# A hybrid attention and SSD layer: the product with V divided by the sums, another interleaving, and row transfers from ScalarE

## The chip, the cores and the metric

The kernel runs on one core of a Trainium2 chip. Its engines work side by side, each on its own queue of instructions in order: TensorE (PE; PEld is its weight load), VectorE (DVE), ScalarE (ACT), GpSimd (POOL) and SyncE (SP), which here only issues transfers. Operands lie in SBUF, the results of TensorE in the eight banks of PSUM. The metric is the device time of one execution in microseconds (us); the kernel before takes 1001.02 us, the median of three runs from 999.69 to 1004.33.

## The reference

One layer of a diffusion backbone: 512 latent tokens and 256 context tokens of width 1024, in float32. The parts that matter here:

```python
def attend(q_nope, q_rope, k_nope, k_rope, v):
    s = (jnp.einsum("bqhd,bkhd->bhqk", q_nope, k_nope)
         + jnp.einsum("bqhr,bkr->bhqk", q_rope, k_rope)) * ATTN_SCALE
    p = jax.nn.softmax(s.astype(jnp.float32), axis=-1).astype(v.dtype)
    return jnp.einsum("bhqk,bkhd->bqhd", p, v)
...
        attn_x = latent_attention(q_nope_x, q_rope_x,
                                  jnp.concatenate([k_nope_c, k_nope_x], axis=1),
                                  jnp.concatenate([kr_c, k_rope_x], axis=1),
                                  jnp.concatenate([v_c, v_x], axis=1))
...
        y_x = ssd_output(st_xf[0], st_xf[1]) + flip(ssd_output(st_xb[0], st_xb[1]))
        ssd_x = ssd_finish(y_x, xs_x, z_x, ssd_d[l], ssd_norm[l])

        mix_x = jnp.concatenate([attn_x, ssd_x], axis=-1) @ w_out[l]
        x = x + mod_x[2] * rms_norm(mix_x, mix_post_norm[l])
        ffn_x = conv_glu(modulate(rms_norm(x, ffn_pre_norm[l]), mod_x[3], mod_x[4]),
                         w_up[l], ffn_conv_w[l], ffn_conv_b[l], w_down[l])
        x = x + mod_x[5] * rms_norm(ffn_x, ffn_post_norm[l])
```

There are 16 heads of attention, 512 queries against 768 keys each, and an SSD (a scan in chunks of 128, in both directions) in two groups of heads; both feed one output projection, and a gated MLP follows.

## The kernel before

Large products are made from pairs of tiles: `split` (L495) rounds an operand to its high part on ScalarE (L497) and takes the rest on VectorE (L498), and three products of the parts stand for one. Tokens are cut in blocks of 128 rows.

The program goes through the input projections (`xbc`, `latent`; `gemm_T` at L751), the SSD (`ssd`, `ssd_finish`), attention in eight pairs of heads (`project`, `pair_of_heads`), the output projection (`natural_gemm`, L1289), the MLP's way up (L751 again) and its way down (L1476).

**SSD.** For each group a recurrence runs over six chunks in two directions: POOL multiplies the inputs by weights (L1005), TensorE multiplies (L1010), POOL multiplies the state of the chunk before by its decay (L1014), VectorE adds (L1015). Then come the masks (L1025 to L1039) and the outputs (L1044 to L1063). `ssd_finish` scales the rows and transposes them (L1082).

**Attention.** `project` makes q, k and v of a pair of heads; SP moves them from partitions to partitions (L1150 to L1156). For each block of 128 queries of a head, `scores` makes 128 x 768 scores in PSUM (L1175), VectorE takes the negative maximum of each row (L1177), ScalarE the exponential and each row's sum (L1179), VectorE the reciprocal of the sum (L1181), POOL multiplies the 768 columns by it (L1182). `transposed` turns the six blocks in PSUM (L1193, two banks) and splits them; `weighted` multiplies with V (L1205), in a form in which the result has the 64 dims of the head on partitions and the queries along the row. That is copied and added into the tile of the pair (L1229, L1230).

**Modulation.** The rows that scale the output projection and the MLP's input come from products with a weight of 1024 x 1024 each (`modblock`, VectorE at L586, eight transfers of 512 KB). `modfinish` has each as a column of 8 values on 128 partitions, writes it to DRAM (L1276, 1024 words) and reads it back as a row, copied to all partitions (L1278). Both transfers are issued by POOL. The first two rows belong to the output projection (`after_mix`, L1354 and L1373), the third to the end.

**Order.** The code is run once to record its instructions, and a planner (`plan`, `Graph`) then orders each engine's instructions by their distance to the end, priced by a table of its own, and gives every tile its place in SBUF: `UNITS` pieces of 256 words per partition, four to a block. A tile's place must be free in the order of the code, and the planner prefers places that came free earlier by `MARGIN`. `beside` (L453) sets the order of the code: it runs the SSD (`group_sums`) as the main line and the projections and attention (`projections`) beside it, and `pace` says how much of the second goes with a given amount of the first. What is left of the second runs alone afterwards.

## Time and profile before

| what | value |
| --- | --- |
| median of three runs | 1001.02 us (999.69 to 1004.33) |
| span of the profiled execution | 994.4 us, 14412 instructions (the page lists no time of its own for it) |
| TensorE clock granted, mean | 0.990 |
| read from HBM, written | 96.02 MB, 4.21 MB |
| GpSimd at L1182 | 64 instructions, 97.3 us |
| ScalarE busy | 501.4 us |

The span goes from the first to the last instruction. A busy engine has an instruction in work; ends of matmuls are modelled, so they overlap, and a busy TensorE is not one at its peak. The granted clock is the share of full speed that TensorE is given. In groups of instructions a row has line, engine, operation, output and inputs by the program's names, shapes, count, busy us, mean ns of one, and the idle time before them with what ended it. In waits a row has who waited for whom, us in total, times, the longest.

### The profile page before, as it was taken

The numbers are of one execution on the slowest core, as the hardware profiler recorded it, in microseconds if no ns is written. First come the engines' busy times: TensorE is split into PE (matmuls) and PEld (weight loads), VectorE is DVE, ScalarE is ACT, GpSimd is POOL, SyncE is SP. The second block draws the span as 40 slices with busy tenths as digits, with TensorE's granted clock in tenths as the row PEclk, the third lists the DMA queues.
The fourth block names the chain that finished last, engine by engine and source line by source line (L and its number), as shares of the span: only waits on it lengthen the run. The fifth ranks groups of instructions, "written<-read, shape, count | busy, mean of one in ns | idle before, by whom it ended". The sixth has DMA issues, their size and how long they took to land.

```text
span 994.4 us, 14412 instructions
## 1 busy us (share of the span) xinstructions
PE 971.8 (98%) x5224; PEld 825.9 (83%) x5224; DVE 700.9 (70%) x1304; ACT 501.4 (50%) x994; POOL 259.5 (26%) x223
## 2 busy tenths in 40 slices
PE   9999999999998999999999999999999999999996
PEld 8888888888876888888888888888888888888885
DVE  5999866988896989978789997952515442773406
ACT  4545337568566787687787324842314323452101
POOL 0001001765697886656541000000000000000000
PEclk7999999999998999999999999999999999999999
DMA  9922101012222242331566965431223221354422
GB/s 350 362 74 85 53 1 44 22 48 81 67 57 54 56 111 78 99 74 46 153 259 230 323 160 199 148 127 64 106 85 106 106 85 43 110 177 137 158 76 84
DMA packets 42214, 116.88 MB, mean 118 GB/s; under 512 B 5776, under 2 KB 8736, under 8 KB 42144
## 3 DMA queue, kind: packets, MB, share of 16 engines
q1 hardware_dynamic: 41440, 114.30, 34.8%
q0 software_dynamic: 528, 1.59, 0.5%
q8 instruction: 41, 0.67, 0.3%
q14 instruction: 29, 0.24, 0.1%
q10 hardware_dynamic: 176, 0.09, 0.0%
HBM read 96.02 MB, written 4.21 MB: 101 GB/s over the span
## 4 chain that ended last, share of the span: by engine, by line
PE 49%; DVE 6%; DMA 4%; issue 2%; ACT 1%; SPq 0%; POOL 0%; DVEq 0%; ACTq 0%; POOLq 0%
PE banks L751 26%; PE banks L1476 12%; PE banks L1175 4%; PE banks L1205 3%; PE banks L1193 2%; DVE block L498 2%; DMA block<-block 1%; DMA mod_rows<-mod 1%; DVE block L586 1%; PE banks L1109 1%; DMA block<-mod_rows 1%; ACT block L1179 1%; DVE smalls L1177 1%; DMA block<-in_wmod_dram 0%; DVE smalls L524 0%
## 5 line engine op out<-in xcount | busy, mean ns | idle before, releaser
L751 PE MATMUL banks<-block,block 128*128 128x512 f32 (+1 forms) x2132 | 448.3, 360 | 1.7 <-DVE block L1385 1.1
L751 PEld LDWEIGHTS banks<-block,block 128*128 128x128 f32 x2132 | 358.8, 188 | 62.5 <-issue 1.6
L498 DVE TENSOR_TENSOR block<-block,block 128x512 fp32r<-128x512 f32 (+5 forms) x252 | 227.0, 923 | 125.7 <-PE banks L751 47.8
L497 ACT ACTIVATE block<-block 128x512 fp32r<-128x512 f32 (+5 forms) x252 | 181.4, 743 | 207.8 <-PE banks L751 48.1
L1476 PE MATMUL banks<-block,block 128*128 128x512 f32 x496 | 116.6, 389 | 0.0
L1182 POOL TENSOR_TENSOR block<-block,smalls 128x768 f32<-128x768 f32 x64 | 97.3, 1527 | 60.7 <-DVE smalls L1181 38.4
L1476 PEld LDWEIGHTS banks<-block,block 128*128 128x128 f32 x496 | 93.0, 188 | 19.5
L1175 PE MATMUL banks<-block,block 128*128 128x512 f32 (+1 forms) x384 | 95.1, 357 | 1.4 <-DMA block<-block 0.7
L1276 POOL DMA_DIRECT2D mod_rows<-mod x3 | 2.9, 975 | 351.4 <-DVE mod L1272 351.4
L498 DVE TENSOR_TENSOR block<-banks,block 128x256 fp32r<-128x256 f32 (+1 forms) x156 | 83.2, 555 | 14.7 <-ACT block L497 12.9
L497 ACT ACTIVATE block<-banks 128x256 fp32r<-128x256 f32 (+1 forms) x156 | 73.0, 498 | 32.4 <-PE banks L1193 17.7
L1289 PE MATMUL banks<-block,block 128*128 128x512 f32 x384 | 88.6, 390 | 0.0
L1289 PEld LDWEIGHTS banks<-block,block 128*128 128x128 f32 x384 | 71.8, 188 | 14.5
L1193 PE MATMUL banks<-cst,block 128*128 128x128 f32 x384 | 66.9, 279 | 4.1 <-DVE block L498 3.7
L1205 PE MATMUL banks<-block,block 128*128 128x256 f32 x384 | 68.7, 299 | 0.8 <-DVE block L498 0.8
L1175 PEld LDWEIGHTS banks<-block,block 128*128 128x128 f32 x384 | 59.6, 190 | 10.2 <-ACT block L1179 2.7
L586 DVE SCALAR_TENSOR_TENSOR block<-block,block 128x1024 f32<-128x1024 f32 x52 | 62.6, 1219 | 4.1 <-DMA block<-in_wmod_dram 1.9
L1177 DVE TENSOR_REDUCE smalls<-banks 128x1 f32<-128x768 f32 x64 | 60.8, 950 | 6.6 <-PE banks L1175 5.9
L1179 ACT ACTIVATE block<-banks,smalls 128x768 f32<-128x768 f32 x64 | 57.7, 902 | 13.2 <-DVE smalls L1177 7.6
L786 DVE SCALAR_TENSOR_TENSOR block<-banks,cwh,block 128x510 f32<-128x510 f32 (+3 forms) x88 | 51.1, 620 | 14.4 <-ACT block L782 13.9
L1205 PEld LDWEIGHTS banks<-block,block 128*128 128x128 f32 x384 | 55.9, 191 | 5.3 <-DVE block L498 1.1
L1193 PEld LDWEIGHTS banks<-cst,block 128*128 128x128 f32 x384 | 47.7, 143 | 14.1 <-DVE block L498 3.9
(216 smaller groups left out, 1064.1 us busy)
## 6 DMA issues: line engine op xcount, KB each, us to landing
block<-in_wmod_dram SPq DMA_DIRECT2D x48, 512.0 KB, 6.9
block<-in_wup_dram SPq DMA_DIRECT2D x44, 512.0 KB, 3.8
block<-in_wdn_dram SPq DMA_DIRECT2D x44, 256.0 KB, 2.8
block<-block SPq DMA_DIRECT2D x32, 256.0 KB, 3.0
block<-in_wout_dram SPq DMA_DIRECT2D x16, 512.0 KB, 5.9
block<-block SPq DMA_DIRECT2D x56, 128.0 KB, 2.3
block<-in_wxbc_dram SPq DMA_DIRECT2D x12, 512.0 KB, 3.4
block<-in_wz_dram SPq DMA_DIRECT2D x16, 256.0 KB, 7.1
```

The costliest lines, as they stand in the source:

```text
L497: act(hi, src, AF.Copy)
L498: (lo_eng or V).tensor_tensor(out=lo, in0=src, in1=hi, op=ALU.subtract)
L586: V.scalar_tensor_tensor(out=junk, in0=wt, scalar=0.5, in1=vec, op0=ALU.mult, op1=ALU.mult, accum_out=acc)
L751: mm(po, lhsT=wf(k, pt[0]), rhs=xf(k, pt[1]), start=(k == 0 and pt == parts[0]), stop=(k == nk - 1 and pt == parts[-1]))
L1175: mm(sc[:, o : o + n], lhsT=q_[:, x_, qi * P : (qi + 1) * P], rhs=kk[:, y_, :], start=part == 0, stop=part == 2)
L1177: V.reduce_max(nm, sc[:, :T], axis=AX.X, negate=True)
L1179: act(pe, sc[:, :T], AF.Exp, bias=nm, scale=1.0, accum_out=sm_)
L1182: G.tensor_tensor(out=pe, in0=pe, in1=sm_.to_broadcast([P, T]), op=ALU.mult)
L1193: nc.tensor.transpose((tx if c < NX else tc_)[:, o : o + P], pe[:, s_ : s_ + P], ident)
L1205: mm(po[:, half * 256 : half * 256 + 256], lhsT=vst(c), rhs=rhs, start=(part == 0 and c == 0), stop=(part == 1 and c == NKT - 1))
L1289: mm(po[i][:, nh * 512 : nh * 512 + 512], lhsT=l[lp][:, i * P : (i + 1) * P], rhs=w[wp][:, nh * 512 : nh * 512 + 512], start=(k == 0 and l ...
L1476: mm(po[i], lhsT=l[lp][:, i * P : (i + 1) * P], rhs=w[wp], start=(k == 0 and lp == 0 and wp == 0), stop=(k == NF - 1 and lp == 1))
```

## The change

```diff
-UNITS, EDGE, MARGIN = 200, 168, 2500
+UNITS, EDGE, MARGIN = 212, 168, 2500
...
+PACE = 1.6
...
-    def scores(qkk, qi):
+    def scores(qkk, qi, sum_):
...
-        nm, sm_ = small("nm"), small("rs")
+        nm = small("nm")
         V.reduce_max(nm, sc[:, :T], axis=AX.X, negate=True)
         pe = t4(P, T)
-        act(pe, sc[:, :T], AF.Exp, bias=nm, scale=1.0, accum_out=sm_)
+        act(pe, sc[:, :T], AF.Exp, bias=nm, scale=1.0, accum_out=sum_)
         pfree(sc)
-        V.reciprocal(out=sm_, in_=sm_)
-        G.tensor_tensor(out=pe, in0=pe, in1=sm_.to_broadcast([P, T]), op=ALU.mult)
         return pe, ox, oc
...
         at = attn[hp // 2][:, hp % 2, :]
+        sums, inv = small("sums", 2 * NX), t2()
+        back = nc.dram_tensor(f"sums_{hp}", (2 * NX, P), F32, kind="Internal").ap()
         for j in range(2):
...
-                    transposed(*scores(heads[j], half * 2 + q2), pT, q2)
+                    transposed(*scores(heads[j], half * 2 + q2, sums[:, j * NX + half * 2 + q2 :][:, :1]), pT, q2)
...
             pfree(po)
+        V.reciprocal(out=sums, in_=sums)
+        with nc.allow_non_contiguous_dma(reason="columns to rows"):
+            nc.sync.dma_start(out=back.rearrange("n p -> p n"), in_=sums)
+        nc.sync.dma_start(out=inv, in_=back.rearrange("(j n) p -> j (n p)", j=2).unsqueeze(1).to_broadcast([2, 64, S]))
+        G.tensor_tensor(out=at, in0=at, in1=inv, op=ALU.mult)
...
-    beside(group_sums(), second, 1.0)
+    beside(group_sums(), second, PACE)
...
-            G.dma_start(out=scratch[n].rearrange("j p -> p j"), in_=ms)
+            nc.scalar.dma_start(out=scratch[n].rearrange("j p -> p j"), in_=ms)
         row = t4()
-        G.dma_start(out=row, in_=scratch[n : n + 1].rearrange("o j p -> o (j p)").to_broadcast([P, D]))
+        nc.scalar.dma_start(out=row, in_=scratch[n : n + 1].rearrange("o j p -> o (j p)").to_broadcast([P, D]))
...
-    nc = bacc.Bacc("TRN2", target_bir_lowering=False, num_devices=1)
+    nc = bacc.Bacc("TRN2", target_bir_lowering=False, num_devices=1, dynamic_dma_scratch_size=4096)
```

The probabilities stay undivided; the eight sums of a pair (two heads of four blocks of queries) are inverted at once, turned into two rows of 512 through DRAM, copied to 64 partitions each, and multiplied into the pair's tile (new lines: reciprocal L1233, write L1235, read L1236, product L1237). The SSD and attention are interleaved at 1.6 units of the second for one of the first, the planner has 212 units in place of 200, and the space that GpSimd's transfers reserve is set to 4096. The modulation's transfers are issued by ScalarE (new L1282, L1284). Below `scores` the new file's lines stand 1 to 6 further down than the old ones.

The planner then orders everything anew. On POOL, where the second group's recurrence meets attention (L1005 and L1014 of the SSD, L1182 the product of the probabilities, L1163 the low part of V), before:

```order
L1182 TENSOR_TENSOR block_373_2457<-block_373_2457,smalls 128x768
L1014 TENSOR_TENSOR block_111_674<-block_193_1374,block_194_1375 128x512
L1182 TENSOR_TENSOR block_311_2167<-block_311_2167,smalls 128x768
L1014 TENSOR_TENSOR block_193_1374<-block_339_2344,block_194_1375 128x512
L1005 TENSOR_TENSOR block_193_1374<-block_228_1617,block_194_1375 128x512
L1182 TENSOR_TENSOR block_386_2527<-block_386_2527,smalls 128x768
L1014 TENSOR_TENSOR block_339_2344<-block_111_674,block_194_1375 128x512
```

And the same place now (L1006, L1015 and L1164 are the old L1005, L1014 and L1163), still on POOL:

```order
L1006 TENSOR_TENSOR block_90_519<-block_223_1598,block_199_1396 128x512
L1015 TENSOR_TENSOR block_439_2886<-block_439_2886,block_199_1396 128x512
L1015 TENSOR_TENSOR block_234_1620<-block_90_519,block_199_1396 128x512
L1015 TENSOR_TENSOR block_263_1837<-block_439_2886,block_199_1396 128x512
L1015 TENSOR_TENSOR block_90_519<-block_234_1620,block_199_1396 128x512
L1006 TENSOR_TENSOR block_231_1611<-block_224_1599,block_199_1396 128x512
L1164 TENSOR_TENSOR block_495_3168<-block_295_2112,block_495_3168 128x2x128
```

The products of the probabilities are gone from between the steps of the recurrence.

On SP, in the middle of attention, where q and k are moved (L1151, L1154 to L1157 are the old L1150, L1153 to L1156; L490 loads a weight), now:

```order
L1157 DMA block_567_3552<-block_57_378 64x512
L1236 DMA block_231_1611<-sums 128x1x512
L1157 DMA block_201_1425<-block_57_378 64x512
L1154 DMA block_622_3906<-block_431_2852 32x1024
L1155 DMA block_622_3906<-block_97_528 32x1024
L1156 DMA block_351_2357<-block_97_528 64x1024
L490 DMA block_477_3089<-in_wk_dram 128x256
L1236 DMA block_231_1611<-sums 128x1x512
L1151 DMA block_622_3906<-block_512_3240 64x1024
L1154 DMA block_512_3240<-block_431_2852 32x1024
L1155 DMA block_512_3240<-block_97_528 32x1024
L1235 DMA sums<-smalls 128x8x1
```

Two reads of rows and a write of sums have come between the moves; the two reads fill the same buffer one after the other. The reads stand apart from their writes, the first of these two 32 rows after it. Of the 16 new transfers the first stands at row 92 of SP's 330, the last at row 210; the last pair's write and read have weight loads between and behind them.

On ScalarE, at the output projection, the modulation's transfers (L1282 writes, L1284 reads back) now stand between splits of weights (L498) and the squares of the projection's rows (L1347):

```order
L498 ACTIVATE block_891_5458<-block_600_3759 128x1024
L1282 DMA mod_rows<-mod 128x8x1
L498 ACTIVATE block_896_5465<-block_600_3759 128x1024
L1282 DMA mod_rows<-mod 128x8x1
L1284 DMA block_804_5113<-mod_rows 128x1024
L498 ACTIVATE block_931_5735<-block_600_3759 128x1024
L1347 ACTIVATE block_814_5155,smalls<-banks 128x1024
L1284 DMA block_839_5260<-mod_rows 128x1024
```

On POOL, before, they stood write, read, write, read behind the last product of the probabilities; now both writes stand ahead of both reads, in the queue of an engine that also splits weights. On TensorE the last product with V and the first product that reads the last pair's output are 209 products of 128x512 apart (by count in the new order).

## The prediction

> **What bounds the kernel now.** I read the page first, then busy time by stage, then what stands in the one stage in which TensorE idles. The page's first line says which engine matters:
>
> ```profile
> PE 971.8 (98%) x5224; PEld 825.9 (83%) x5224; DVE 700.9 (70%) x1304; ACT 501.4 (50%) x994; POOL 259.5 (26%) x223
> ```
>
> TensorE is bound over the whole span, so a gain has to be found where it waits or runs at a lower clock. The table of stages gives stretch, its length, then busy us and instructions of PE, PEld, DVE, ACT and POOL, granted clock, DMA share and GB/s:
>
> ```profile
> 150.00:275.00 125.00, 124.28 (x712) 104.71 (x711) 104.67 (x167) 81.82 (x184) 71.03 (x59) 1.00 0.18 54
> 275.00:400.00 125.00, 116.74 (x677) 97.08 (x675) 108.86 (x196) 93.04 (x229) 102.06 (x85) 0.97 0.27 70
> 400.00:525.00 125.00, 122.83 (x840) 108.13 (x839) 104.85 (x210) 100.06 (x215) 71.32 (x55) 1.00 0.43 125
> 525.00:600.00 75.00, 75.00 (x364) 63.07 (x362) 69.05 (x123) 28.58 (x43) 6.04 (x6) 1.00 0.78 254
> 600.00:650.00 50.00, 48.44 (x288) 42.67 (x287) 43.23 (x118) 30.26 (x64) 1.78 (x1) 1.00 0.43 147
> 650.00:994.40 344.40, 336.75 (x1558) 281.02 (x1556) 148.49 (x235) 101.51 (x153) 1.50 (x2) 1.00 0.30 106
> ```
>
> Attention lies in the second and third stretch. In the second TensorE idles 125 - 116.74 = 8.3 us, and the clock falls below 1; in the third it idles 2.2 us, from 525 to 600 not at all, from 600 to 650 1.6 us. (The 7.7 us of the last stretch lie at the end of the program.) The loss of clock is two records:
>
> ```profile
> 302.20:305.60 3.40, 3.40 (x15) 2.86 (x14) 1.28 (x3) 1.36 (x3) 3.40 (x3) 0.50 0.00 0
> 312.40:315.80 3.40, 3.09 (x12) 2.83 (x13) 2.18 (x6) 2.61 (x7) 2.10 (x2) 0.50 0.09 27
> ```
>
> At half clock 6.8 us do the work of 3.4, so 3.4 us are lost. Why there? POOL is busy 102 of 125 us, more than in any other stretch, and the timeline shows who stands behind whom (start, duration, engine, line; in brackets the idle time before it):
>
> ```profile
> 298.65 1.48 POOL L1014 TENSOR_TENSOR block<-block,block 128x512 f32<-128x512 f32 x1
> 299.99 0.94 PE L1010 MATMUL banks<-block,block 128*128 128x512 f32 x3 [1.51 <-DVE block L1015]
> 300.10 1.91 POOL L1182 TENSOR_TENSOR block<-block,smalls 128x768 f32<-128x768 f32 x1
> 301.87 0.93 PE L1010 MATMUL banks<-block,block 128*128 128x512 f32 x2 [0.94 <-DVE block L1015]
> 301.97 1.04 POOL L1014 TENSOR_TENSOR block<-block,block 128x512 f32<-128x512 f32 x1
> 302.98 2.89 POOL L1182 TENSOR_TENSOR block<-block,smalls 128x768 f32<-128x768 f32 x2
> ```
>
> The SSD recurrence (POOL L1014, then DVE L1015, then the next L1014) shares POOL's queue with the products of the probabilities (L1182). L1014 starts at 301.97 when the L1182 of 300.10 ends; TensorE idles 1.5 and 0.9 us round it, and the first half-clock record follows.
>
> Idle time leaves out short stalls. I count the third stretch to see how many there are:
>
> ```profile
> L1205 PE MATMUL banks<-block,block 128*128 128x256 f32 x239 | 42.7, 300 | 0.0
> L1193 PE MATMUL banks<-cst,block 128*128 128x128 f32 x239 | 41.5, 274 | 1.5 <-DVE block L498 1.4
> L1175 PE MATMUL banks<-block,block 128*128 128x512 f32 x108 | 35.4, 413 | 0.3 <-DMA block<-block 0.3
> L751 PE MATMUL banks<-block,block 128*128 128x512 f32 x69 | 22.9, 409 | 0.0
> L1175 PE MATMUL banks<-block,block 128*128 128x256 f32 x105 | 20.3, 299 | 0.4 <-DMA block<-block 0.4
> ```
>
> The step from matmul to matmul, where nothing is waited for, comes from three rows: the tail of the chain for 512 columns, two merged rows of the timeline for 256 and 128:
>
> ```profile
> 877.88 108.21 PE banks L1476 x477
> 319.51 1.72 PE L1205 MATMUL banks<-block,block 128*128 128x256 f32 x13
> 326.19 0.71 PE L1193 MATMUL banks<-cst,block 128*128 128x128 f32 x5
> ```
>
> 108.21 / 477 = 0.227 us; (1.72 - 0.30) / 12 = 0.12; (0.71 - 0.27) / 4 = 0.11, one matmul's own mean taken off. So 177 x 0.227 + 344 x 0.12 + 239 x 0.11 = 107.8 us for 760 matmuls, 119.1 for all 840: 5.9 us of 125 are stalls, 2.2 of them shown as idle. With the same 3.7 us of short ones the second stretch has 8.3 + 3.4 + 3.7 = 15.4. **The pot** is 15.4 + 5.9 + 1.6 = 22.9 us.
>
> **The change part by part.** What is taken away and what comes:
>
> ```profile
> L1182 POOL TENSOR_TENSOR block<-block,smalls 128x768 f32<-128x768 f32 x64 | 97.3, 1527 | 60.7 <-DVE smalls L1181 38.4 <-PE banks L1193 9.8 <-PE banks L1205 3.8
> L1181 DVE RECIPROCAL smalls<-smalls 128x1 f32<-128x1 f32 x64 | 9.6, 156 | 10.3 <-ACT block L1179 9.8
> L923 DVE RECIPROCAL block<-block 128x192 f32<-128x192 f32 x1 | 1.3, 1343 | 0.0
> L1054 POOL TENSOR_TENSOR block<-block,block 128x512 f32<-128x512 f32 x16 | 25.9, 1617 | 10.7 <-DVE block L1052 8.7 <-DVE smalls L521 1.7
> L1014 POOL TENSOR_TENSOR block<-block,block 128x512 f32<-128x512 f32 x16 | 19.1, 1194 | 9.1 <-DVE block L498 4.5 <-DVE block L1015 3.9 <-ACT block L1012 0.7
> ```
>
> POOL loses 97.3 us and gets 8 products of 128x512 at 1.2 to 1.6 us, 10 to 13 us. DVE loses 64 reciprocals (9.6 us) and gets 8 of eight columns, between 0.16 and 1.3 us each; I take 0.2, near the one-column row: 1.6 us. Per tile, scores to transposes are shorter by 0.16 + 1.53 us and two handovers.
>
> **Term a, the jam.** Of L1182 this much lies in the second stretch:
>
> ```profile
> L1182 POOL TENSOR_TENSOR block<-block,smalls 128x768 f32<-128x768 f32 x25 | 39.7, 1593 | 11.4 <-DVE smalls L1181 6.9 <-DVE smalls L528 1.9 <-PE banks L1029 1.6
> ```
>
> Without these 40 us POOL would be busy 62 of 125, less than the 71 of the third stretch today. So I let the second stretch fall to the third's idle time at full clock: (8.3 + 3.4) - 2.2 = 9.5 us. Bounds: 0, if the recurrence is as late for other reasons, and 15.4.
>
> **Term b, the third stretch.** SSD work moves into it (PACE), L1182 leaves it. Whom TensorE waits for directly is small:
>
> ```profile
> PEld banks L1193 <- DVE block L498: 3.9, 9, 0.7
> PEld banks L1193 <- POOL block L1182: 1.6, 2, 1.3
> ```
>
> The transposes wait for the split of the tile before (L498, which empties their PSUM banks) longer than for L1182. That stays. I take 1.5 of the 5.9 us, near the 1.6 of L1182's own row. The ends are +5.9 and -9.5: in the worst case the SSD work that now stands there makes the third stretch what the second is today.
>
> **Term c, rows of the modulation on ScalarE.** The wait for the second transfer of each pair on POOL:
>
> ```profile
> 581.68 0.57 POOL L1278 DMA_DIRECT2D block<-mod_rows  x1 [10.79 <-DMA mod_rows<-mod]
> 595.09 0.56 POOL L1278 DMA_DIRECT2D block<-mod_rows  x1 [9.73 <-DMA mod_rows<-mod]
> ```
>
> Today the second row leaves only after the first has been sent and read, one after the other; in the new order both writes stand ahead of both reads on ScalarE, so one round of 10 us overlaps the other, and the stretch 600 to 650, whose idle time follows the late row, gives back 1.0 of its 1.6 us. ScalarE waits for the landing in its own queue; it idles more than half of 525 to 600 (28.58 of 75 busy), which covers up to 10 us. If that cover were gone, the weight splits behind it would be 10 us late and the term -10 at worst, which ends at 1000. The Trainium skill ("DMA: Bandwidth & Descriptors", section "Issuing engines are not separate DMA queues") says that issuing from another engine saves only the sequencer's time. By it this term would be 0, not 1.0, and the forecast 990.0; the two landings above, 10 us whoever waits, speak for it, the changed order against.
>
> **Costs of the row of sums.** Eight writes of 1024 words and eight reads of 256 KB join SP's queue. The nearest rows:
>
> ```profile
> mod_rows<-mod POOLq DMA_DIRECT2D x3, 4.0 KB, 10.3
> block<-mod_rows POOLq DMA_DIRECT2D x3, 512.0 KB, 7.2
> block<-block SPq DMA_DIRECT2D x56, 128.0 KB, 2.3
> ```
>
> 10.3 + 7.2 us from sums to rows, with 1.3 to 1.6 for the product: about 19 us. It is hidden for all but the last pair by the pairs that follow. For the last, 209 products of 128x512 stand in the new order between the last product with V and the first that reads its output: 209 x 0.227 = 47 us, so 28 us remain. Were the cover gone, 19 us would show. Issue on SP, at the 0.57 us of POOL's two rows above, is 16 x 0.57 = 9 us of a queue that mostly waits. I take 0; the other end is the third rival. The 12 units (three blocks of 4 KB per partition) and the smaller scratch are memory that the planner spends; no instruction of their own, cost 0.
>
> **Sum:** 9.5 + 1.5 + 1.0 = 12.0 us off the profiled span of 994.4, so 982.4. The page gives no time of its own for that execution; the median of the runs, 1001.02, lies 6.6 us over the span, and I keep these: 982.4 + 6.6 = **989.0 us**. With the whole pot: 971.5 + 6.6 = 978; a shorter chain could also help the splits, so I let the lower end reach 974.
>
> **Rivals.** *Nothing much changes.* The transposes are limited by two PSUM banks and the splits, and the half clock stays, because the recurrence still alternates between POOL and DVE. For it: TensorE waits for L1182 1.6 us in all. Against: POOL at 82% just where the clock falls. Only the direct wait and some idle time go: 3 us, 998.0.
>
> *The row reads hold SP.* A read (L1236) waits for its write to land and, since the rows share a buffer, for the product before it (L1237); SP is in order, and behind it stand the moves of q and k that the next scores need. Such moves are on the chain today:
>
> ```profile
> 443.05 2.22 DMA block<-block
> 473.06 4.04 DMA block<-block
> ```
>
> Seven pairs are followed by others. From 12.0 / 7 = 1.7 us a pair the gain is gone, from 2.4 the kernel is slower by 0.5%. One read of 7.2 us, half hidden, costs 3.6 a pair: 7 x 3.6 = 25.2, so 989.0 + 25.2 = 1014. For it: two reads stand amid the moves with five and more moves close behind. Against: the first waits for a write sent 32 rows earlier; in rows 174 to 210 mostly weights follow, which are loaded ahead.
>
> *The jam moves* (the change does not do what it says): the second stretch gains 9.5 us and the third, which takes over SSD work, loses 9.5. Left is term c, 1001.0 - 1.0 = 1000.0. For it: DVE, which the recurrence needs as well, is busy 105 of 125 us there already. Against: POOL has 97 us more for both.
>
> **Chances.** A measurement tells about 0.5% from no change, so faster means under 996, slower over 1006. Forecast (974 to 995) 0.70; nothing much 0.13; the jam moves 0.07; SP held 0.10. Faster 0.70, same 0.20, slower 0.10. The range for 8 in 10 runs from 974 to 1004: it takes in both rivals without a change and leaves out the slow one.
>
> **What would show it.** Attention today reaches from the first scores to the last product with V:
>
> ```profile
> L1175 PE MATMUL banks<-block,block x384: 277/388/796, 273.5 to 525.4; 128*128 128x512 f32 x126, 128*128 128x256 f32 x66
> L1205 PE MATMUL banks<-block,block x384: 274/282/681, 287.0 to 534.1; 128*128 128x256 f32 x192
> ```
>
> Right, term a: POOL near 259.5 - 97.3 + 11.5 = 174 us busy, less the issue of the row transfers; a granted clock of 1.00 in every stretch from 150 to 650; these 260.6 us some 11 us shorter. Term b: TensorE's idle time in its second half about 2 us. Term c: no idle TensorE after the products of the output projection. Wrong: scores waiting for DMA block<-block by more than 10 us in all, SP waiting at L1236, ScalarE waiting at L1284 while weight splits are late, or L1010 still waiting for DVE L1015 at a half-clock record.

## The result, and the profile after

The changed kernel took 1028.02 us (median of 4 runs, 1022.29 to 1030.42) beside 1000.36 us for the kernel before: a ratio of 1.025, 95% interval 1.0213 to 1.0286. The forecast was 989.0 us in a range of 974 to 1004. The change makes the kernel slower by 2.5%.

The page of the changed kernel, with the span, busy time by engine, and the packets of all transfers:

```profile
span 1024.5 us, 14216 instructions
...
PE 977.8 (95%) x5224; PEld 831.5 (81%) x5224; DVE 691.0 (67%) x1248; ACT 497.8 (49%) x992; POOL 162.7 (16%) x161
...
DMA packets 54597, 119.01 MB, mean 116 GB/s; under 512 B 17136, under 2 KB 20096, under 8 KB 54528
```

The 97.3 us of L1182 are gone from POOL and the eight products with the rows (L1237) take 10.8, as forecast; POOL's 162.7 us are 11 below the forecast 174, which still held the 4.6 of issuing transfers. TensorE does the same 5224 matmuls, and the span is 30.1 us longer. The stretches of the prediction, after the change:

```profile
150.00:275.00 125.00, 122.80 (x683) 101.05 (x682) 94.08 (x150) 69.81 (x154) 50.38 (x44) 1.00 0.18 51
275.00:400.00 125.00, 121.05 (x761) 104.35 (x760) 103.13 (x165) 99.79 (x246) 60.47 (x59) 1.00 0.34 71
400.00:525.00 125.00, 104.35 (x652) 90.81 (x652) 93.31 (x181) 83.56 (x192) 40.86 (x38) 0.92 0.45 106
525.00:600.00 75.00, 72.72 (x403) 61.94 (x402) 65.99 (x101) 41.04 (x72) 4.35 (x3) 1.00 0.72 228
600.00:650.00 50.00, 43.39 (x199) 35.87 (x197) 34.16 (x91) 12.63 (x23) 1.27 (x1) 0.96 0.76 204
```

275 to 400 us is better than before, as forecast: 761 matmuls in place of 677, full clock. 400 to 525 is far worse: 652 in place of 840, TensorE idle 20.7 us, and the clock falls. The records at half clock now lie here and after attention:

```profile
441.20:451.40 10.20, 5.49 (x17) 4.20 (x18) 1.89 (x3) 1.59 (x4) 0.70 (x2) 0.50 0.00 0
506.10:509.50 3.40, 3.40 (x15) 3.09 (x14) 2.20 (x4) 2.60 (x6) 0.00 (x0) 0.50 0.20 34
516.30:523.10 6.80, 4.27 (x19) 3.87 (x20) 4.73 (x9) 2.11 (x5) 0.00 (x0) 0.50 0.90 296
646.00:656.20 10.20, 6.36 (x28) 6.07 (x29) 9.72 (x35) 6.79 (x22) 1.27 (x1) 0.50 0.38 146
```

What stands ahead of the first of these? The timeline of the changed kernel (start, duration, engine, line; idle time before it and its end in brackets):

```profile
437.77 0.49 SPq L1156 DMA_DIRECT2D block<-block  x1
...
438.36 0.55 SPq L1157 DMA_DIRECT2D block<-block  x1
...
438.95 0.59 SPq L1235 DMA_DIRECT2D sums<-smalls  x1
...
442.72 1.65 PE L1176 MATMUL banks<-block,block 128*128 128x512 f32 x3 [4.28 <-DMA block<-block]
...
447.56 0.80 PE L1176 MATMUL banks<-block,block 128*128 128x256 f32 x2 [3.19 <-DMA block<-block]
```

SP issues two moves of q and k, and 0.6 us behind them the write of the sums' reciprocals as 1024 words. The scores wait for the moves until 442.7 and 447.6. The transfers of that stretch (436 to 450 us in 40 slices of 0.35 us, tenths busy, then GB/s):

```profile
DMA  2411000089778910000000000000000000000000
GB/s 20 59 29 12 3 0 0 0 176 199 293 275 160 20 24 12 0 0 0 0 0 0 0 0 0 0 0 0 0 0 0 0 0 0 0 0 0 0 0 0
DMA packets 1257, 0.45 MB, mean 32 GB/s; under 512 B 1086, under 2 KB 1128, under 8 KB 1256
```

The last packet of these transfers starts at 441.8 us. For 5.7 us more TensorE still waits for a move to be reported as landed.

The modulation rows show a like delay on ScalarE's queue:

```profile
593.30 0.40 ACTq L1282 DMA_DIRECT2D mod_rows<-mod  x1
...
601.73 0.38 ACTq L1282 DMA_DIRECT2D mod_rows<-mod  x1
...
605.02 0.34 ACTq L1284 DMA_DIRECT2D block<-mod_rows  x1
...
621.11 0.34 ACTq L1284 DMA_DIRECT2D block<-mod_rows  x1
...
621.50 1.06 ACT L498 ACTIVATE block<-block 128x1024 fp32r<-128x1024 f32 x1 [5.74 <-DMA mod_rows<-mod]
...
647.20 1.23 PE L752 MATMUL banks<-block,block 128*128 128x256 f32 x4 [5.03 <-ACT block L1390]
```

The reads follow their writes by 11.7 and 19.4 us, a weight split stands behind them for 5.7 us, and at 647 TensorE has waited 5.0 us for what follows from the row.

To compare runs I add up, over all matmul starts of a trace, how much longer each step to the next is than the undisturbed step for its columns (0.227 us for 512, 0.117 for 256, 0.109 for 128). Time lost to half clock is in these sums, and the step taken for the few narrower matmuls makes them uncertain by about 2 us. In us, with three of the experiments below:

| stretch | before | after | both_runs | turned_frozen | turned_split |
| --- | --- | --- | --- | --- | --- |
| 150 to 275 | 8.0 | 10.9 | 10.3 | 10.9 | 10.3 |
| 275 to 400 | 21.9 | 10.6 | 9.1 | 9.4 | 9.5 |
| 400 to 525 | 9.2 | 34.4 | 19.1 | 20.1 | 15.2 |
| 525 to 600 | 0.3 | 4.2 | 0.2 | 1.9 | 0.2 |
| 600 to 675 | 3.5 | 11.4 | 2.7 | 2.7 | 2.7 |

### The profile page after: what moved, and what is told of

The parts are those of the page before. It is cut to its first block, busy times and chain, and to the rows that moved or that the text cites. A ratio compares the mean times of both kernels' runs of the same rounds, so it can differ in the third digit from the quotient of the medians.

```text
span 1024.5 us, 14216 instructions
## 1 busy us (share of the span) xinstructions
PE 977.8 (95%) x5224; PEld 831.5 (81%) x5224; DVE 691.0 (67%) x1248; ACT 497.8 (49%) x992; POOL 162.7 (16%) x161
## 2 busy tenths in 40 slices
DMA packets 54597, 119.01 MB, mean 116 GB/s; under 512 B 17136, under 2 KB 20096, under 8 KB 54528
## 4 chain that ended last, share of the span: by engine, by line
PE 77%; DMA 9%; DVE 9%; ACT 2%; issue 2%; SPq 1%; POOL 0%; DVEq 0%; ACTq 0%; POOLq 0%
PE banks L752 40%; PE banks L1482 12%; PE banks L685 5%; PE banks L1176 4%; DVE block L499 3%; PE banks L1204 3%; DMA block<-in_wmod_dram 2%; PE banks L1192 2%; DMA block<-in_wout_dram 2%; DMA mod_rows<-mod 2%; PE banks L1110 2%; DMA block<-block 2%; PE banks L1059 1%; DVE block L587 1%; PE banks L1051 1%
## 5 line engine op out<-in xcount | busy, mean ns | idle before, releaser
L752 PE MATMUL banks<-block,block 128*128 128x512 f32 (+1 forms) x2132 | 453.9, 363 | 9.7 <-ACT block L1390 5.0
L752 PEld LDWEIGHTS banks<-block,block 128*128 128x128 f32 x2132 | 362.2, 190 | 71.3 <-ACT block L1390 5.3
L498 ACT ACTIVATE block<-block 128x512 fp32r<-128x512 f32 (+6 forms) x252 | 180.8, 744 | 209.2 <-PE banks L752 58.9
L499 DVE TENSOR_TENSOR block<-block,block 128x512 fp32r<-128x512 f32 (+4 forms) x252 | 221.2, 903 | 89.4 <-ACT block L498 51.2
L1482 PE MATMUL banks<-block,block 128*128 128x512 f32 x504 | 118.5, 389 | 0.0
L1176 PE MATMUL banks<-block,block 128*128 128x512 f32 (+1 forms) x384 | 100.5, 365 | 15.6 <-DMA block<-block 8.1
L1482 PEld LDWEIGHTS banks<-block,block 128*128 128x128 f32 x504 | 94.6, 188 | 19.6
L499 DVE TENSOR_TENSOR block<-banks,block 128x512 fp32r<-128x512 f32 (+1 forms) x156 | 84.1, 556 | 18.7 <-ACT block L498 17.3
L498 ACT ACTIVATE block<-banks 128x512 fp32r<-128x512 f32 (+1 forms) x156 | 75.9, 501 | 29.6 <-PE banks L1192 19.9
L1295 PE MATMUL banks<-block,block 128*128 128x512 f32 x384 | 89.7, 391 | 0.0
L1176 PEld LDWEIGHTS banks<-block,block 128*128 128x128 f32 x384 | 62.1, 194 | 26.5 <-ACT block L1180 10.1
L1295 PEld LDWEIGHTS banks<-block,block 128*128 128x128 f32 x384 | 71.5, 188 | 14.7 <-DVE block L1231 0.3
L1204 PEld LDWEIGHTS banks<-block,block 128*128 128x128 f32 x384 | 58.2, 195 | 6.4 <-issue 2.0
L1427 DVE TENSOR_TENSOR block<-banks,block 128x512 f32<-128x512 f32 x22 | 15.2, 690 | 66.3 <-PE banks L752 65.0
L685 PE MATMUL banks<-block,block 128*128 128x512 f32 x192 | 54.2, 408 | 0.0
```

The lines of the kernel that those rows point to most:

```text
L498: act(hi, src, AF.Copy)
L499: (lo_eng or V).tensor_tensor(out=lo, in0=src, in1=hi, op=ALU.subtract)
L685: mm(po[i], lhsT=hx[k][:, hp, i * P : (i + 1) * P], rhs=wz[wp], start=(k == 0 and wp == 0 and hp == 0), stop=(k == KD - 1 and hp == 1))
L752: mm(po, lhsT=wf(k, pt[0]), rhs=xf(k, pt[1]), start=(k == 0 and pt == parts[0]), stop=(k == nk - 1 and pt == parts[-1]))
L1176: mm(sc[:, o : o + n], lhsT=q_[:, x_, qi * P : (qi + 1) * P], rhs=kk[:, y_, :], start=part == 0, stop=part == 2)
L1204: mm(po[:, half * 256 : half * 256 + 256], lhsT=vst(c), rhs=rhs, start=(part == 0 and c == 0), stop=(part == 1 and c == NKT - 1))
```

## The experiments

The planner orders everything anew after nearly any edit, so most runs keep an order that exists: the recording run, from which the plan is made, sees the old code (`places is None`) or the old price, and only the program that runs has the edit. Instructions that are added stay outside the plan. Ratios, with their 95% intervals, are to the kernel before, run beside each group; its median lies between 998.4 and 1002.5 us there, so differences between medians of different groups are good to a few us.

### The words taken away, in the changed order

**sums_runs** (the same edit for `scratch[n]` and `ms`, L1282, is **mod_runs**; **both_runs** has both):

```diff
-            nc.sync.dma_start(out=back.rearrange("n p -> p n"), in_=sums)
+            nc.sync.dma_start(out=back.rearrange("n p -> (n p)").rearrange("(p n) -> p n", n=2 * NX), in_=sums)
```

> The changed kernel with the same order on every engine; only the write of the sums' reciprocals (L1235) puts each partition's 8 values side by side in DRAM (128 runs of 32 bytes instead of 1024 single words). The turning of columns into rows is left out by it, so the values that L1237 multiplies by are not the reference's. Theory 'words' (the 1024 words are done late and hold up the q/k moves and loads that were issued around them): the third stretch (400-525 us) gets back most of what it lost against before, 104 us of PE busy towards 115, no q/k move of L1156/L1157 lands over 3 us after its issue, and the time is 1006 to 1016 us (12 to 22 below the changed kernel). Rival 'order' (the new plan itself starves TensorE there, whatever the writes cost): 1024 to 1030 us, PE busy in 400-525 stays at 104. Rival 'SP held' (SP stands at the read L1236 until the write has landed): the same drop as 'words', but it would go with a fall of SP's waiting at L1236, which the changed kernel's trace would have to show first.

> The changed kernel with the same order on every engine; only the modulation columns (L1282) are written as 128 runs of 32 bytes, the turning of columns into rows is left out by it. Theory 'words': the two rows at 593 and 602 us, read 12 and 19 us after their writes in the changed kernel, are read 3 to 5 us after them, the 5.0 and 2.7 us gaps of PE at 642 and 648 go with the half clock behind them, and the time is 1016 to 1022 us (6 to 12 below the changed kernel). Rival 'order': 1024 to 1030 us with the gaps at 642 to 651 still there, since something else than the row is late.

> The changed kernel with the same order on every engine and both edits of the two runs before (sums and modulation written in runs of 32 bytes, the turning left out). Theory 'words': both drops add up, 992 to 1004 us, so that the change without the word writes is level with the kernel before or a little below it; half clock in 400-655 us no more than 4 us in all (15 us before in the changed kernel's records). Rival 'order': 1022 to 1030 us.

Measured: sums_runs 1000.29 us (ratio 1.0025, 0.9999 to 1.0051), mod_runs 1016.73 (1.0173, 1.014 to 1.0206), both_runs 997.9 (0.9976, 0.994 to 1.0013). Against the 1028.02 us of the changed kernel, with each instruction in its place, the form of eleven writes of 4 KB is worth 30 us: 28 for the sums (more than the 12 to 22 that I expected), 11 for the modulation, less than the sum of both when together. The bytes are the same. "Order" falls, since the order didn't change. The stage of sums_runs, its waits for moves (9.8 us in the changed kernel by the row among the signs further down), and the landing in both_runs (bytes of one transfer, then median us from issue to landing):

```profile
400.00:525.00 125.00, 115.71 (x756) 101.51 (x755) 107.06 (x201) 97.82 (x222) 41.25 (x39) 0.97 0.47 135
```

```profile
PEld banks L1176 <- DMA block<-block: 0.9, 2, 0.5
```

```profile
sums<-smalls SPq DMA_DIRECT2D x8, 4.0 KB, 2.0
```

2.0 us to land. But 115.7 busy us are not yet the 122.8 of before: something else is left.

### Another queue, other packets

**both_soft** issues the word writes from POOL, in the order of the plan:

```diff
-            nc.sync.dma_start(out=back.rearrange("n p -> p n"), in_=sums)
+            (nc.sync if places is None else G).dma_start(out=back.rearrange("n p -> p n"), in_=sums)
```

and likewise L1282 and L1284.

> The changed kernel with the same planned order of PE, DVE and SP; the sums' write L1235 and both modulation transfers L1282/L1284 are issued by POOL instead of SP and ScalarE, the output is the reference's. In the kernel before the same kind of column written from POOL went as 16 packets of 256 bytes and landed in 5 to 11 us. Theory 'words': fewer and larger packets free the q/k moves and loads, 996 to 1010 us. Rival 'SP held': SP still stands at L1236 until the write has landed, so 1020 to 1030 us. Rival 'order': 1022 to 1032 us.

Measured: 1027.56 us (1.0284, 1.0234 to 1.0334). The forecast by "words" was wrong. The page shows fewer packets, 17136 - 6048 = 11088 or 11 x (1024 - 16) under 512 bytes, so 16 for each write. Yet the landing did not shorten: the median is 10.5 us, where such writes from POOL landed in 8.7 to 11.2 us in the kernel before (not 5 to 11, as I had it). Packets, issues and timeline of both_soft:

```profile
DMA packets 43509, 119.01 MB, mean 116 GB/s; under 512 B 6048, under 2 KB 9008, under 8 KB 43440
```

```profile
sums<-smalls POOLq DMA_DIRECT2D x8, 4.0 KB, 10.5
```

```profile
440.15 0.90 POOL L1235 DMA_DIRECT2D sums<-smalls  x1 [0.45 <-issue]
...
440.46 0.48 SPq L1157 DMA_DIRECT2D block<-block  x1
...
451.31 1.01 PE L1176 MATMUL banks<-block,block 128*128 128x256 f32 x3 [9.25 <-DMA block<-block]
```

The scores wait for a move from SP's queue, issued 0.3 us behind a write from POOL's, until 10.9 us after its issue. So a transfer on another queue than the write's is late too, and the number of packets on the page does not show it. "SP held", whose numbers this run met, falls with the next group, where nothing reads what is written; and SP's own waits at the reads are too short for it in the changed kernel (4.0 us in 400 to 530, 6.6 in the whole run):

```profile
SPq L1236 <- DMA block<-sums: 2.7, 1, 2.7
...
SPq L1236 <- POOL block L1237: 1.3, 1, 1.3
```

### The words put into the kernel before

**before_words** (**before_extra_runs** writes the same bytes in the form of sums_runs), with a tensor that nobody reads:

```diff
+        if places is not None:
+            extra = nc.dram_tensor(f"extra_{hp}", (2 * NX, P), F32, kind="Internal").ap()
+            with nc.allow_non_contiguous_dma(reason="columns to rows"):
+                nc.sync.dma_start(out=extra.rearrange("n p -> p n"), in_=at[:, : 2 * NX])
```

> The kernel before, with the same planned order on every engine, and one more transfer for each pair of heads: SP writes 8 columns of the finished attention tile (128x8) as 1024 single words into a DRAM tensor that nothing reads. Theory 'words': each write takes some 10 us to land, transfers issued within a few us of it land late too, TensorE waits for q/k moves or loads as in the changed kernel: 1008 to 1022 us. Rival 'new order' (the words hurt only the changed kernel, whose plan leaves its moves no slack): 998 to 1004 us.

> As the run before, with the same 4 KB written as 128 runs of 32 bytes. Both theories: the writes land in about 2 us and the time is that of the kernel before, 997 to 1003 us; anything above says that an eighth more SP transfers cost by themselves.

Measured: 1013.3 us (1.0121, 1.0079 to 1.0163) with words, 1001.09 (0.9994, 0.9957 to 1.0031) with runs, both as "words" has it; "new order" falls. The same place in both, words first:

```profile
371.74 0.39 SPq L1235 DMA_DIRECT2D extra<-block  x1
...
372.17 0.71 SPq L489 DMA_DIRECT2D block<-in_wv_dram  x1
...
381.54 0.63 ACT L497 ACTIVATE block<-block 128x512 fp32r<-128x512 f32 x1 [5.89 <-DMA block<-in_wv_dram]
```

```profile
370.70 0.33 SPq L1235 DMA_DIRECT2D extra<-block  x1
...
371.08 0.45 SPq L489 DMA_DIRECT2D block<-in_wv_dram  x1
...
375.24 0.63 ACT L497 ACTIVATE block<-block 128x512 fp32r<-128x512 f32 x1 [0.63 <-DMA block<-in_wv_dram]
```

A load of a weight, issued 0.4 us behind the write, is used 9.4 us after its issue beside words and 4.2 beside runs. This shows the cause without the change around it, at less than half of the 28 us: what a write costs depends on what is issued near it.

**sums_pairs** asks what sets the time to land. The turning is half left out:

```diff
-                nc.sync.dma_start(out=back.rearrange("n p -> p n"), in_=sums)
+                nc.sync.dma_start(out=back.rearrange("n p -> (n p)").rearrange("(a p k) -> p a k", a=NX, k=2),
+                                  in_=sums.rearrange("p (a k) -> p a k", k=2))
```

> The changed kernel with the same order on every engine; the write of the sums' reciprocals goes as 512 pieces of 8 bytes, so half of the turning is left out and the values that L1237 multiplies by are not all the reference's. If the time to land goes by the number of pieces (10.3 us for 1024, 2.0 us for 128 of 32 bytes), it is 5 to 6.5 us here, TensorE's waits of 4 us for q/k moves at 438 and 501 us shrink to 0 to 2 us, and the time is 1004 to 1018 us. If it goes by the size alone (anything under some tens of bytes is equally slow), it lands in 9 us or more and the time stays at 1022 to 1030 us.

Measured: 1001.04 us (0.9991, 0.9955 to 1.0027):

```profile
sums<-smalls SPq DMA_DIRECT2D x8, 4.0 KB, 4.8
```

About 10.5 us for 1024 pieces (medians from 9.0 in late_alone to 11.6 in before_words), 4.8 for 512, 2.0 for 128: it falls with the number of pieces. Each piece grows as their number falls (4, 8, 32 bytes), so the two are not told apart. 4.8 us already cost little here: the time is that of sums_runs, under both of my ranges.

### The parts of the change alone

**rest_alone** is the kernel before with `PACE = 1.6`, 212 units, the smaller scratch and the modulation rows on ScalarE; **late_alone** is the late division with none of these. Both are planned anew. **rest_turned** and **before_turned** turn the modulation columns ahead of their writes (the function is shown below), in the orders of rest_alone and of before.

> The kernel before with all of the change but the late division: PACE 1.6, 212 units with the smaller DMA scratch, the modulation rows issued by ScalarE; the probabilities are still divided by POOL. It is planned anew, so every queue has another order. If the interleaving is what costs in 400-525 us, this loses there too: 1008 to 1020 us. If the words of the sums are what costs, it stays within 992 to 1008 us.

> The kernel before with the late division alone (sums turned through DRAM by word writes, product on POOL; PACE 1.0, 200 units, modulation rows on POOL), planned anew. Theory 'words': the 10 us that the jam on POOL is worth are gained in 275-400 us and 15 to 25 lost later, 1005 to 1022 us. Rival 'interleaving' (PACE 1.6 is what costs): 985 to 997 us.

> All of the change but the late division in its own plan's order (1002 us), with the modulation columns turned by VectorE outside the plan and written by ScalarE in runs of 128 bytes, the reference's output. Its stalls in 600-675 us were 12.2 us where the kernel before has 3.5. Theory 'words': they fall to 2 to 4 us, 990 to 996 us, faster than the kernel before. Rival 'ScalarE's queue' (the transfers stand behind activations there): 999 to 1004 us.

> The kernel before in its order, with only its three modulation columns (POOL) turned by VectorE and written in runs of 128 bytes. Theory 'words': no more than its 3.5 us of stalls in 600-675 us are there to gain, 996 to 1002 us.

Measured: rest_alone 1002.19 us (0.9989, 0.996 to 1.0019), late_alone 1060.23 (1.0577, 1.0527 to 1.0626), rest_turned 993.45 (0.9948, 0.9912 to 0.9984), before_turned 998.2 (1.0007, 0.9982 to 1.0033). The interleaving does not cost what the change lost; the late division does, in another order twice as much, 1060 us being far outside both of my ranges. In rest_alone stalls fall from 21.9 to 15.6 us in 275 to 400 and rise from 3.5 to 12.2 in 600 to 675; turning the columns takes the latter to 6.1, more than I expected to remain, and the kernel is then 0.5% faster than before. In before_turned there was nothing to gain: the same words cost nothing there.

### Turning on VectorE, and what was left

**turned_frozen** keeps the changed order. VectorE turns blocks of 32 by 32 ahead of each write of a column, which then goes as 128 runs of 128 bytes:

```diff
+    def rowwise(q, dst, src):
+        if places is None:
...
+        V.tensor_copy(turnc[:, :8], src)
+        V.transpose(out=turnr, in_=turnc)
+        q.dma_start(out=dst.rearrange("j (b p) -> b j p", b=4), in_=turnr)
...
-        with nc.allow_non_contiguous_dma(reason="columns to rows"):
-            nc.sync.dma_start(out=back.rearrange("n p -> p n"), in_=sums)
+        rowwise(nc.sync, back, sums)
```

**turned_dve2** and **late_turned** tell the planner of it (the latter without the rest of the change); **late_frozen** does it in the order of late_alone.

> The changed kernel with the planned order kept on every engine, and the reference's output: ahead of each column write VectorE copies the 8 columns into a 128x32 tile and turns it in blocks of 32 by 32, so that the write goes as 128 runs of 128 bytes (22 short VectorE instructions more, for the sums and for the modulation). Theory 'words': as the run with both columns in runs, 992 to 1004 us, writes landing in about 2 us. If the turning or another transfer costs, 1006 to 1020 us.

> The same turning by VectorE, but known to the planner, so with an order of its own. Theory 'words': no wait of TensorE for q/k moves over 3 us at a column write, 985 to 1004 us. If the changed kernel's parameters (PACE 1.6 with 212 units) are what lets TensorE starve in 400-525 us, 1004 to 1020 us.

> The kernel before with the late division alone (PACE 1.0, 200 units, modulation rows on POOL), both kinds of columns turned by VectorE and written in runs of 128 bytes, planned anew. Theory 'words': the 58 us that the late division alone lost go with the word writes, 985 to 1003 us. If its plan is what loses them, 1030 to 1060 us as there.

> The late division alone in the order that its own plan gave (1060 us with word writes), with both kinds of columns turned by VectorE outside the plan and written in runs of 128 bytes. Theory 'words': two gaps of 10 to 11 us and the smaller ones behind q/k moves go, 1000 to 1020 us. If the plan is what loses the 58 us: 1040 to 1060 us.

Measured: turned_frozen 999.82 us (0.9967, 0.9935 to 0.9998), turned_dve2 1016.69 (1.0125, 1.008 to 1.017), late_turned 1015.05 (1.0103, 1.0056 to 1.015), late_frozen 1029.42 (1.0269, 1.0175 to 1.0363). Turned_frozen came as expected; late_turned and late_frozen fell between the ranges of both theories, and turned_dve2 into that of PACE and the units, against which late_turned speaks, as slow without them. The words were 31 of the 58 us that late_alone lost. Every order with the late division kept 19 us of stalls or more in 400 to 525, against 9 to 10 in the orders without it.

**norow** took POOL's wait for the row away, on both_runs; the kernel leaves the division by the sums out:

```diff
-        G.tensor_tensor(out=at, in0=at, in1=inv, op=ALU.mult)
+        G.tensor_tensor(out=at, in0=at, in1=inv if places is None else ones[:, :1].to_broadcast([P, S]), op=ALU.mult)
```

> The run with both columns in runs of 32 bytes, with the same order, and the product L1237 takes a tile of ones in place of the row of reciprocals: the division by the sums is left out, the row is still written and read. It tells what the wait for the row (37 us of POOL's waiting between 400 and 525 us) is worth. Theory 'the row holds POOL and its block': TensorE's stalls in 400-525 us fall from 19 to 9 or 12 us as before, 986 to 993 us. Rival 'the plan' (the exp's and the q/k moves' blocks come free late whatever POOL does): 995 to 1001 us, the gap of 4.7 us at 486 us still there.

Measured: 996.64 us (0.9969, 0.9941 to 0.9997), stalls of 18.6 us in 400 to 525. POOL's wait is not it, as the rival had it. But the row was still read. The timeline of late_frozen, whose order has the worst place, and the busy times of 3.7 us within it:

```profile
480.40 0.56 SPq L1248 DMA_DIRECT2D block<-sums  x1
481.06 0.51 SPq L1169 DMA_DIRECT2D block<-block  x1
481.66 1.20 SPq L1170 DMA_DIRECT2D block<-block  x2
488.81 1.26 POOL L1249 TENSOR_TENSOR block<-block,block 128x512 f32<-128x512 f32 x1 [6.89 <-DMA block<-sums]
...
490.21 1.19 PE L1189 MATMUL banks<-block,block 128*128 128x512 f32 x2 [10.38 <-DMA block<-block]
```

```profile
484.80:488.50 3.70, 0.00 (x0) 0.00 (x0) 0.00 (x0) 0.00 (x0) 0.00 (x0) 0.50 0.13 48
```

All five engines stand still, and of 16 DMA engines a share of 0.13 is busy: two. From the issue of the read to POOL's product with the row it takes 8.4 us, and the scores wait 1.4 us longer still, for one of the moves issued from 0.7 us behind the read on.

**turned_split** and **late_split** (on turned_frozen and late_frozen) issue each read in two halves:

```diff
-        nc.sync.dma_start(out=inv, in_=back[: 2 * NX].rearrange("(j n) p -> j (n p)", j=2).unsqueeze(1).to_broadcast([2, 64, S]))
...
+            for j in range(2):
+                nc.sync.dma_start(out=inv[64 * j : 64 * j + 64],
+                                  in_=back[NX * j : NX * j + NX].rearrange("(o n) p -> o (n p)", o=1).to_broadcast([64, S]))
...
```

> The changed kernel in its order with the columns turned by VectorE (999.8 us), and each read of a row (L1236, 256 KB whose outermost dimension is 2) issued as two transfers of 64 partitions, one behind the other. In the run with both columns in runs of 32 bytes the packets of such a read ran never more than two or three at a time and took 6.2 us, and a q/k move issued behind it ended only at 486.3, 7 us after its issue. Theory 'reads on two DMA engines': with 64 partitions outermost the read spreads, lands in 3 us or less, POOL's waits for it and the q/k moves' lateness go, stalls in 400-525 us fall from 20 to 9 to 12 us: 986 to 994 us, faster than the kernel before. Rival 'the plan' (blocks come free late for other reasons): 997 to 1002 us.

> The late division alone in its own order, columns turned by VectorE (1029 us), with the reads split in the same way. There SP stood at the read until POOL's product had freed the block, and scores waited 10.4 us for a move issued 0.7 us behind a read. Theory 'reads on two DMA engines': that gap and the like of it go, 1003 to 1015 us. Rival 'the plan': 1022 to 1030 us.

Measured: turned_split 993.57 us (0.9921, 0.9891 to 0.9952), late_split 998.89 (0.9971, 0.9936 to 1.0005), 31 us under late_frozen and better than I expected. "The plan" falls in both orders. Not all came as "reads on two DMA engines" had it: the stalls of turned_split in 400 to 525 fell to 15.2 us, not to 9 to 12, a half lands in 5.0 us by the median of late_split, not in 3, and POOL still waits 40.7 us for the rows in turned_split. What went are waits behind moves. In late_frozen the scores wait 18.7 us for moves, in late_split 2.2. In turned_frozen the exponentials wait for moves and TensorE for the exponentials (the first two rows, 400 to 530 us; the third is turned_split, where the exponentials wait for no move):

```profile
ACT block L1193 <- DMA block<-block: 5.7, 2, 4.7
PE banks L1189 <- ACT block L1193: 6.0, 3, 4.4
```

```profile
PE banks L1189 <- ACT block L1193: 0.4, 2, 0.2
```

SP's waits at the reads fall as well, from 4.6 to 0.6 us and from 12.7 to 4.0 in the late orders, so how much of the gain is a queue that stands and how much are transfers that land late was not told apart. The stages of turned_split, 0.8% faster than the kernel before:

```profile
275.00:400.00 125.00, 122.70 (x771) 105.33 (x770) 105.89 (x174) 101.21 (x248) 61.00 (x60) 1.00 0.29 73
400.00:525.00 125.00, 118.34 (x793) 103.74 (x793) 114.84 (x221) 102.95 (x234) 42.93 (x40) 1.00 0.51 146
525.00:600.00 75.00, 75.00 (x357) 62.83 (x356) 64.43 (x118) 25.89 (x37) 2.38 (x1) 1.00 0.71 248
600.00:650.00 50.00, 49.42 (x320) 44.58 (x320) 43.73 (x118) 30.28 (x63) 1.28 (x1) 1.00 0.45 150
```

## Why the prediction was wrong

**Costs of the row of sums: this step failed.** I wrote "I take 0", because a cover of 47 us hides the row, and asked only who waits for the row. That cover held: TensorE idles 0.0 us at the products of the output projection (L1295), and POOL's waits for the rows cost nothing that norow shows. What I left out is which transfers are late beside those of the row. The writes cost 28 us in the changed order (sums_runs) and the reads 6 more (999.82 to 993.57 us, turned_frozen to turned_split). The row that I quoted, 10.3 us for 4 KB beside 2.3 us for 128 KB, was the warning: a transfer with a thirtieth of the bytes and four times the landing is late for something else than its bytes, and the nearest transfers are late with it.

On the words the Trainium skill ("DMA: Bandwidth & Descriptors", section "Queues, rings and completion order") says that a DMA engine's report of completion lands only after all earlier writes of that engine, across its queues. The trace agrees: the move that the scores waited 9.25 us for in both_soft was on SP's queue, behind words on POOL's. It is not the whole account: in the changed kernel both moves were issued ahead of the words, by 0.6 and 1.2 us, and were late all the same, and where the 5.7 us without a packet go no run here shows. I had cited the Trainium skill for term c and did not ask it about the sums.

**The row reads hold SP** (1014, 0.10) was the rival on the right side, for a wrong reason in the changed kernel: SP waited 6.6 us at the reads, 4.0 of them by the two rows above, and the writes alone are 28 of the loss. What the read keeps busy are the two DMA engines that carry it; in the order of late_frozen SP did stand at its reads, 12.7 us. I took 7.2 us for a read; in late_frozen it was 8.4. The Trainium skill ("DMA: Bandwidth & Descriptors", section "Rules for kernel authors") says that an outermost dimension below 16, a broadcast of few copies for instance, confines a transfer to at most as many DMA engines. The read's outermost dimension is 2, and 0.13 of 16 is 2.1: the trace agrees.

**Term a, the jam: right in size, its cause shown in part.** 9.5 us forecast; stalls in 275 to 400 fell from 21.9 to 10.6, 11.3 us, and the clock stayed at 1.00. But either half of the change lowers them alone: to 15.6 in rest_alone, where POOL still spends 39.6 us of that stretch at L1182, and to some 13 in late_split, at the old pace. So a part of what I put down to POOL's queue comes from the interleaving.

**Term b, the third stretch: wrong sign.** Minus 1.5 forecast, in bounds from 5.9 gained to 9.5 lost. With words and slow reads gone, stalls are 15.2 against 9.2: 6.0 us more, inside the bounds, on the side of "the jam moves". SSD work does stand there now (8 products of the masks on POOL, L1039, none before), and the transposes wait 3.8 us for the splits ahead of them, 1.4 before. That this is the reason for the 6 us was not tried.

**Term c, the modulation on ScalarE: mis-sized.** 1.0 us gained was forecast, with 10 lost as the other end. 7.9 were lost (3.5 to 11.4). The cover that I named failed as described, ScalarE standing 5.7 us at the landing while a weight split was due, but the size comes from the words: turned, the same place has 2.7 us, 0.8 under before, near the forecast's 1.0. That the words go from ScalarE and not from POOL is no cause: both_soft sends them from POOL and is as slow.

**The sum.** Without both faults of the transfers the changed kernel takes 993.57 us, 4.6 above the forecast and in its range. That it comes so near is in part luck: term b is 7.5 us off and 150 to 275 loses 2.3, against 2.9 us more from term a, all in stalls. The form of eleven writes and eight reads cost 34 us (1028.02 to 993.57). That the late division itself gains is not shown: rest_turned, where POOL still divides, takes 993.45 us (ratio 0.9948 beside 0.9921, intervals that overlap), and late_split, the late division without the rest, 998.89, with an interval that holds 1.

**The signs I had named.** Of those for "wrong" the waits of the changed kernel show two, the scores a little under my 10 us:

```profile
PEld banks L1176 <- DMA block<-block: 9.8, 4, 4.5
...
ACT block L498 <- DMA mod_rows<-mod: 5.7, 1, 5.7
```

SP stood at L1236 for the 6.6 us named above, and TensorE no longer waits for the recurrence at a half-clock record. Two signs for "right" failed: the clock is 0.92 in 400 to 525 and 0.96 in 600 to 650, and attention, from the first scores to the last product with V, takes 290.6 us (267.2 to 557.8) in place of 260.6. A list that had asked for transfers that land late, with no engine named, would have caught the reads as well.

## What to carry to other kernels

Price a small transfer by its pieces and by the number of DMA engines that carry it, and charge it to the transfers issued around it (0.3 to 1.2 us away in the places shown), not only to whoever reads it. Turn a column into a row on an engine before it is written, and put a long dimension outermost in a broadcast read. Where a planner reorders all after any edit, test an edit in the frozen order first: the same turning by VectorE in two orders differed by 17 us here (turned_frozen, turned_dve2).

## What the runs showed of the hardware

Times to land for 4 KB were 2.0, 4.8 and about 10.5 us for 128, 512 and 1024 pieces: near 0.011 us for each piece between the last two, an estimate from 4.8 and 10.5. 1024 pieces written by POOL appear as 16 packets of 256 bytes in place of 1024 of 4, and land no sooner (10.5 us in both_soft, 11.6 from SP in before_words). The turn of 128x32 values on VectorE is cheap (turned_frozen: busy us, mean ns of one):

```profile
L1107 DVE STREAM_TRANSPOSE turnr<-turnc 128x32 f32<-128x32 f32 x11 | 2.3, 207 | 0.1
```

Half clock came with the stalls: between 150 and 660 us its records last 30.6 us in the changed kernel, 6.8 before and 3.4 in turned_split. If TensorE does half the work in them, 15.3, 3.4 and 1.7 us are lost, an estimate.
